# An mLSTM over a sequence of two chunks: the second chunk reads the first by its scores, without a state

## The chip, the core and the metric

The kernel runs on one core of one Trainium2 chip. A core has five engines that run side by side, each with its own list of instructions: TensorE (PE, matmuls into the accumulation memory PSUM), VectorE (DVE), ScalarE (ACT), GpSimd (POOL), and SyncE (SP), which here issues the transfers between the chip's main memory and the on-chip memory. Instructions of one engine run in order; engines wait for each other by semaphores. The metric is the device time of one execution in microseconds (us), the median of several.

## The reference, cut to what matters

One encoder layer is computed for two separate sequences, `x_prompt` with 1024 rows and `x_sample` with 256 rows, all in float32. Its second branch is an mLSTM in both directions with 4 heads of 256 channels. The sequence is cut into chunks of 128 rows; a state `C` (256x256) and `n` (256) is carried from chunk to chunk:

```python
def body(carry, inp):
    C, n, m = carry
    ...
    S = jnp.einsum('bhtd,bhsd->bhts', qc, kc) * Dexp
    num = jnp.einsum('bhts,bhsd->bhtd', S, vc) + inter_w[..., None] * jnp.einsum('bhtd,bhde->bhte', qc, C)
    den_raw = jnp.sum(S, axis=-1) + inter_w * jnp.einsum('bhtd,bhd->bht', qc, n)
    ...
    C_new = decay[..., None, None] * C + jnp.einsum('bhs,bhsd,bhse->bhde', w, kc, vc)
    n_new = decay[..., None] * n + jnp.einsum('bhs,bhsd->bhd', w, kc)
    return (C_new, n_new, m_new), h
```

The state starts at zero in each sequence and direction. `x_prompt` has 8 chunks, `x_sample` has 2. So in the short sequence only one state is ever used: the one that the first chunk leaves, read once by the second. There `qc` times `C_new` is `q (sum over s of w_s k_s v_s)`, which is the same number as `sum over s of (q k_s) w_s v_s`.

## The kernel before, in words

The kernel has three stages: the input projections (line 770, up to about 1168 us of the trace), the mLSTM stage (about 1168 to 1457 us), and the output projections (lines 1530 to 1532 and 1742 to 1744).

In the mLSTM stage the ten chunks are numbered 0 to 7 (long sequence) and 8, 9 (short). `qT`, `kT` hold q and k by channel (transposed), `vN` holds v by rows with a column of ones and one of zeros added (258 columns, so that `n` rides along), each in three pieces: chunks 0 to 4, 5 to 7, and 8, 9. Rows of k are loaded once more by chunk into small tiles `k` (six buffers).

A `Sweep` is one head in one direction. For every chunk it first takes a query, then makes a state:

- `query` (line 1357): two matmuls, q of the chunk times the state C, into the PSUM tile `qc` (one buffer); ACT scales it into `kept` or `qcf`.
- `state` (lines 1369 to 1383): a load of the rows of k, a scaling of v on ACT into `wv` (four buffers), two matmuls k times wv into the PSUM tile `u` (one buffer, line 1375), and on DVE a copy (line 1381, first state of a sequence) or decay and sum (line 1383) into the next C.

Two sweeps run per head: the first one's queries are kept, the second one runs ten steps later together with `Pairs`, which makes the scores inside a chunk (line 1418), weights and normalizes them, multiplies them with v (line 1458), transposes the result (line 1505), gates it into `og` on DVE (line 1508) and stores it to `ym_dr`. Heads 0 and 1 begin their first sweep with the short sequence (chunk 9, then 8), heads 2 and 3 end it there.

Between these small matmuls a `Filler` puts the matmuls of another product (lines 1597 to 1599, tiles `acc`): 32 units of 24 matmuls with 320 columns, each unit closed by a DVE step (line 589) that needs a tile `th`, loaded from `th_dr`. Two units can be open at a time.

The order of all this is not written out by hand. Each operation is recorded on a `Board` with an engine, a cost in us, what it reads and writes, and a step; `order` then plays a greedy list schedule over these costs, and every engine, SP with its loads among them, gets its instructions in that order. So a change in recorded operations can move others. Transfers all go through SP's queue.

Near the end of the stage `first_ym` loads parts of `ym_dr` back into `th` tiles and splits them for the next stage (ACT line 1618, DVE line 1619, tiles `y`).

Of the kernel before, what the change touches and what calls it, by code (L numbers as in the profile page):

```python
# [9 lines left out]
F32 = mybir.dt.float32  # L10
# [171 lines left out]
def encoder_kernel(  # L182
# [1153 lines left out]
    class Sweep:  # L1336


        def __init__(self, h, d, p):
            self.h, self.d, self.i, self.p, self.C = h, d, h % 2, p, None  # L1340
            self.order, self.first, self.has_state, self.has_query = [], set(), set(), set()
            for c0, n in SEQS[::1 - 2 * d]:
                cs = list(range(c0, c0 + n))[::1 - 2 * d]
                self.order += cs
                self.has_state.update(cs[:-1])
                self.has_query.update(cs[1:])
                self.first.add(cs[0])

        def query(self, c, dst, tok):
            if c not in self.has_query:  # L1350
                return
            i, C = self.i, self.C
            pq = buf(psM, [P, 512], F32, "qc", 1)

            def mm():
                for kd in range(2):
                    PE.matmul(pq[:, 0:HD + 2], qTs[i][:, kd, c * P:(c + 1) * P], C[:, kd, :], start=kd == 0, stop=kd == 1)  # L1357

            op("PE", .88, mm, r=[(qTs[i], piece(c)), C], w=[pq])
            op("ACT", .47, lambda: A.activation(dst(), pq[:, 0:HD + 2], AF.Copy, bias=0.0,  # L1360
                                                scale=gcol[:, 1, self.d, self.h, c:c + 1]), r=[pq], w=[tok])

        def state(self, c):
            if c not in self.has_state:
                return
            i, n, h = self.i, piece(c), self.h
            k, wv = buf(mp_, [P, HD], F32, "k", 6), buf(mp_, [P, HD + 2], F32, "wv", 4)
            load(128, lambda: k[:], kn_dr[c * P:(c + 1) * P, h * HD:(h + 1) * HD], (), [k])
            op("ACT", .51, lambda: A.activation(wv[:], vNs[i][:, c, :], AF.Copy, bias=0.0,
                                                scale=gcol[:, 3, self.d, h, c:c + 1]), r=[(vNs[i], n)], w=[wv])  # L1370
            pu = buf(psM, [P, 2, 512], F32, "u", 1)

            def mm():
                for db in range(2):
                    PE.matmul(pu[:, db, 0:HD + 2], k[:, db * P:(db + 1) * P], wv[:], start=True, stop=True)  # L1375

            op("PE", .88, mm, r=[k, wv], w=[pu])
            C0 = self.C
            C1 = self.C = buf(mp_, [P, 2, HD + 2], F32, f"C{self.p}", 2)
            if c in self.first:  # L1380
                op("DVE", .7, lambda: V.tensor_copy(C1[:], pu[:, :, 0:HD + 2]), r=[pu], w=[C1])
            else:
                op("DVE", .76, lambda: V.scalar_tensor_tensor(
                    out=C1[:], in0=C0[:], scalar=decay[:, self.d, h, c:c + 1], in1=pu[:, :, 0:HD + 2],
                    op0=ALU.mult, op1=ALU.add), r=[pu, C0], w=[C1])
# [251 lines left out]
    for s in range(10 * NH + 15):  # L1637
        board.step = s
        if s == 0:
            fills.unit(())  # L1640
            load_head(0, 2, "v")
        h, c, i = second(s - 3)
        if h is not None and h + 2 < NH and c in (5, 7, 9):
            load_head(h + 2, (5, 7, 9).index(c))
        h, i = divmod(s, 10)
        mark = len(board.ops)
        if h < NH:
            c, d = one[h].order[i], one[h].d
            one[h].query(c, lambda h=h, c=c, d=d: kept[h % 2][:, slot(d, c), :], (kept[h % 2], c))
            one[h].state(c)  # L1650
        if s == 0:
            fills.unit(())
            for n in DOWN:
                load_head(0, n, "q" if n == 2 else "qv")
            fills.unit(())
            fills.unit(())
        h, c, i = second(s)
        if h is not None:
            g = c - c % 2
            if i % 2 == 0:  # L1660
                prs[h, g] = Pairs(h, g, two_[h].d)
            two_[h].query(c, *prs[h, g].inter(c))
            two_[h].state(c)
            prs[h, g].scores(c)
            if i % 2:
                prs[h, g].factors()
        h, c, i = second(s - 2)
        if h is not None:
            prs[h, c - c % 2].values(c)
        h, c, i = second(s - 4)  # L1670
        if h is not None and i % 2 == 0:
            prs[h, c - c % 2].finish()
        if s in (3, 5):
            for h, n in ((0, 0), (1, 2), (1, 1)) if s == 3 else ((1, 0), (0, 1), (0, 2)):
                load_head(h, n, "qkv" if h else "k")
        after = [o for o in board.ops[mark:] if o.eng == "PE"][:1]
        while fills.at < PACE[s]:
            fills.unit(after)
        if s == 45:
            ym0 = [first_ym(0)]  # L1680
# [175 lines left out]
```

## Time and profile before

| | us |
|---|---|
| device time, median of 3 | 1698.51 |
| lowest, highest | 1695.8, 1698.83 |
| span of the profiled execution, first to last instruction | 1694.4 |
| PE busy in that span | 1654.8 |
| DVE, ACT, POOL busy | 1000.7, 577.4, 678.6 |

The profile is one execution; its own device time is not listed beside its span. A row of a group of instructions reads: line, engine, operation, output tile <- input tiles, shape, count, then busy us and mean ns of one, then the idle time of the engine just before them and what ended it. A float32 matmul shows as two records, so "x4" at a query is one query of two matmuls. A row of the timeline reads: start, duration, engine, line, operation, and in brackets the idle time of the engine before it with what ended that. DMA stands for a transfer, SPq for its issue.

### The profile page before, as it was taken

What the parts mean: (1) busy time and instruction counts of PE and PEld (TensorE: products, weight loads), DVE (VectorE), ACT (ScalarE), POOL (GpSimd) and SP (SyncE); (2) the same over time, 40 slices, a digit from 0 to 9 for tenths busy, and PEclk for the clock granted to TensorE, in tenths of its full rate; (3) what the DMA queues carried; (4) which work ended last, traced back from release to release, by engine and by line L of the source; (5) the groups of instructions that cost most, each with busy time, mean ns of one, the idle gap of its engine ahead of it and who ended that gap; (6) DMA issues with size and microseconds to landing.
All of it is one profiled execution on the core that took longest, in us unless ns stands there. A gap on an engine that the chain in (4) does not pass through costs nothing.

```text
span 1694.4 us, 27722 instructions
## 1 busy us (share of the span) xinstructions
PE 1654.8 (98%) x10542; PEld 1567.3 (92%) x10542; DVE 1000.7 (59%) x1696; ACT 577.4 (34%) x1117; POOL 678.6 (40%) x499
## 2 busy tenths in 40 slices
PE   7999999999999999999999999999999999999997
PEld 2799999999999999999999999999988899998985
DVE  4794434456555565566656886652267777565645
ACT  3552332124453222222222211212256565333322
POOL 1133333335664566677666633333210101223412
PEclk9999999999999999999999999999999999999999
DMA  9334325324553122221222556468779855783631
GB/s 318 108 127 137 120 89 124 73 77 124 149 154 103 57 69 69 82 81 61 62 66 82 145 129 141 118 134 289 254 234 293 261 186 158 231 279 119 239 108 63
DMA packets 282681, 241.88 MB, mean 143 GB/s; under 512 B 96196, under 2 KB 237748, under 8 KB 282548
## 3 DMA queue, kind: packets, MB, share of 16 engines
q1 hardware_dynamic: 282368, 240.06, 46.6%
q8 instruction: 84, 1.38, 0.3%
q14 instruction: 49, 0.40, 0.1%
q10 hardware_dynamic: 180, 0.04, 0.0%
HBM read 171.16 MB, written 68.89 MB: 142 GB/s over the span
## 4 chain that ended last, share of the span: by engine, by line
PE 90%; DVE 4%; DMA 3%; SPq 1%; issue 1%; ACT 1%; ACTq 0%; DVEq 0%
PE acc L770 61%; PE qc L1357 3%; PE u L1375 3%; PE accd L1530 2%; PE accd L1531 2%; PE accd L1532 2%; PE accd L1743 2%; PE accd L1744 2%; PE accd L1742 2%; PE acc L1598 2%; PE acc L1597 2%; PE acc L1599 2%; DMA raw<-in_w_in_dram 1%; PE misc L1418 1%; SPq L318 1%; PE misc L1458 1%
## 5 line engine op out<-in xcount | busy, mean ns | idle before, releaser
L330 POOL TENSOR_TENSOR wl<-comb,wh 128x512 fp32r<-128x512 f32 x176 | 247.3, 1405 | 288.0 <-ACT wh L329 279.8
L686 DVE TENSOR_TENSOR q<-acc,q 128x640 f32<-128x640 f32 x272 | 220.8, 819 | 221.5 <-PE acc L770 219.3
L330 POOL TENSOR_TENSOR wl<-raw,wh 128x512 fp32r<-128x512 f32 x136 | 191.8, 1411 | 237.0 <-ACT wh L329 225.2
L770 PE MATMUL acc<-xt,wh 128*128 128x320 f32 x1408 | 265.1, 310 | 2.2 <-DVE xt L382 2.2
L770 PEld LDWEIGHTS acc<-xt,wh 128*128 128x128 f32 x1408 | 220.9, 188 | 3.5 <-DVE xt L382 3.2
L329 ACT CAST wh<-comb 128x512 fp32r<-128x512 f32 x176 | 109.0, 619 | 298.5 <-PE acc L770 282.6
L329 ACT CAST wh<-raw 128x512 fp32r<-128x512 f32 x136 | 84.4, 621 | 271.0 <-PE acc L770 205.5
L770 PE MATMUL acc<-xt,wl 128*128 128x320 f32 x704 | 160.3, 309 | 0.0
L1558 POOL TENSOR_TENSOR wl<-raw,wh 128x512 fp32r<-128x512 f32 x28 | 36.2, 1297 | 233.4 <-ACT wh L1557 227.0
L770 PEld LDWEIGHTS acc<-xt,wl 128*128 128x128 f32 x704 | 117.7, 188 | 0.0
L642 DVE TENSOR_TENSOR comb<-raw 128x512 f32<-128x512 f32 x88 | 73.4, 834 | 41.1 <-DMA raw<-in_w_in_dram 19.1
L837 POOL TENSOR_TENSOR big<-big,q 128x640 f32<-128x640 f32 x48 | 78.3, 1631 | 35.8 <-DVE q L686 27.4
L586 ACT ACTIVATE q<-q,zero 128x640 f32<-128x640 f32 x76 | 63.1, 831 | 78.0 <-DVE q L686 72.3
L642 DVE TENSOR_TENSOR comb<-raw,comb 128x512 f32<-128x512 f32 x44 | 46.0, 1045 | 62.6 <-POOL wl L330 62.6
L770 PE MATMUL acc<-b00H,wh 128*128 128x320 f32 x352 | 81.6, 312 | 0.0
L1530 PE MATMUL accd<-y,wh 128*128 128x320 f32 x256 | 79.9, 313 | 1.5 <-DVE og L1508 1.5
L770 PE MATMUL acc<-b10H,wh 128*128 128x320 f32 x352 | 80.2, 308 | 0.8 <-ACT q L700 0.8
L770 PE MATMUL acc<-b11H,wh 128*128 128x320 f32 x352 | 80.7, 310 | 0.0
L770 PE MATMUL acc<-t2H,wh 128*128 128x320 f32 x352 | 80.4, 310 | 0.0
L770 PE MATMUL acc<-t3H,wh 128*128 128x320 f32 x352 | 80.3, 309 | 0.0
L770 PE MATMUL acc<-t3L,wh 128*128 128x320 f32 x352 | 80.2, 309 | 0.0
L770 PE MATMUL acc<-t3H,wl 128*128 128x320 f32 x352 | 80.2, 309 | 0.0
(307 smaller groups left out, 4144.0 us busy)
## 6 DMA issues: line engine op xcount, KB each, us to landing
raw<-in_w_in_dram SPq DMA_DIRECT2D x108, 256.0 KB
raw<-in_w_in_dram SPq DMA_DIRECT2D x40, 512.0 KB
th<-th_dr SPq DMA_DIRECT2D x32, 320.0 KB
th_dr<-q SPq DMA_DIRECT2D x28, 320.0 KB
raw<-in_w_proj_conv_dram SPq DMA_DIRECT2D x16, 512.0 KB
k<-kn_dr SPq DMA_DIRECT2D x64, 128.0 KB
raw<-in_w_proj_mlstm_dram SPq DMA_DIRECT2D x16, 512.0 KB
raw<-in_w_out_dram SPq DMA_DIRECT2D x16, 512.0 KB
```

The costliest lines, as they stand in the source:

```text
L329: op("ACT", .63, lambda: A.copy(wh[:], src()), r=r, w=[wh])
L330: op("POOL", 1.4, lambda: G.tensor_tensor(out=wl[:], in0=src(), in1=fp(wh[:]), op=ALU.subtract), r=[*r, wh], w=[wl])
L586: A.activation(out, in_, AF.Tanh, bias=zero[:, 0:1], scale=0.5)
L642: op("DVE", .9, lambda: V.tensor_tensor(out=t[:], in0=x(), in1=y(), op=o), r=[x.tok, y.tok], w=[t])
L686: op("DVE", .82, lambda: V.tensor_tensor(out=two(dst()), in0=acc[:, :, 0:TQ], in1=two(t()), op=ALU.add), r=[acc, t.tok], w=[dst.tok])
L770: PE.matmul(acc[:, q, 0:TQ], st_[:, k_, :], m_[:, q * TQ:(q + 1) * TQ], start=k_ == 0 and n == 0, stop=k_ == 3 and n == 2)
L837: op("POOL", 1.65, lambda: G.tensor_tensor(out=dst(), in0=dst(), in1=t(), op=ALU.mult), r=[dst.tok, t.tok], w=[dst.tok])
L1357: PE.matmul(pq[:, 0:HD + 2], qTs[i][:, kd, c * P:(c + 1) * P], C[:, kd, :], start=kd == 0, stop=kd == 1)
L1375: PE.matmul(pu[:, db, 0:HD + 2], k[:, db * P:(db + 1) * P], wv[:], start=True, stop=True)
L1530: PE.matmul(accs[q][:, :TQ], wh, yH, start=kt == 0, stop=False)
L1531: PE.matmul(accs[q][:, :TQ], wh, yL, start=False, stop=False)
L1558: op("POOL", 1.36, lambda wh=wh, wl=wl, src=src: G.tensor_tensor(out=wl[:], in0=src(), in1=fp(wh[:]), op=ALU.subtract), r=[raw, wh], w=[wl])
```

## The change

For the sequence of two chunks, in each head and direction, the state is no longer made. Where the first chunk made it, `crossed` multiplies k of this chunk with q of the other one (two matmuls with 128 columns, accumulated in the PSUM tile `u`), and ACT scales the rows of this score matrix by the weights w of the keys while it copies it into a `wv` buffer, 128 columns wide. The second chunk's query is then one matmul of these weighted scores with v of the first chunk, 258 columns, into `qc`. The load of the rows of k, the scaling of v and the DVE copy go, for this sequence. The loads of head 0 at the start of the stage change with it: all of q, k and v of chunks 8 and 9 come first.

```diff
+                if n == 2:
+                    self.short = cs
 
         def query(self, c, dst, tok):
...
-            op("PE", .88, mm, r=[(qTs[i], piece(c)), C], w=[pq])
+            if c == self.short[1]:
+                w, c0 = self.w, self.short[0]
+                op("PE", .46, lambda: PE.matmul(pq[:, 0:HD + 2], w[:, 0:P], vNs[i][:, c0, :], start=True, stop=True),
+                   r=[w, (vNs[i], piece(c0))], w=[pq])
+            else:
+                op("PE", .88, mm, r=[(qTs[i], piece(c)), C], w=[pq])
...
+        def crossed(self, c):
+
+            i, t = self.i, self.short[1]
+            pu, self.w = buf(psM, [P, 2, 512], F32, "u", 1), buf(mp_, [P, HD + 2], F32, "wv", 4)
+            w = self.w
+
+            def mm():
+                for kd in range(2):
+                    PE.matmul(pu[:, 0, 0:P], kTs[i][:, kd, c * P:(c + 1) * P], qTs[i][:, kd, t * P:(t + 1) * P],
+                              start=kd == 0, stop=kd == 1)
+
+            op("PE", .45, mm, r=[(kTs[i], piece(c)), (qTs[i], piece(t))], w=[pu])
+            op("ACT", .29, lambda: A.activation(w[:, 0:P], pu[:, 0, 0:P], AF.Copy, bias=0.0,
+                                                scale=gcol[:, 3, self.d, self.h, c:c + 1]), r=[pu], w=[w])
 
         def state(self, c):
             if c not in self.has_state:
                 return
+            if c == self.short[0]:
+                return self.crossed(c)
...
         if s == 0:
             fills.unit(())
-            load_head(0, 2, "v")
+            load_head(0, 2)
...
-            for n in DOWN:
-                load_head(0, n, "q" if n == 2 else "qv")
+            for n in DOWN[1:]:
+                load_head(0, n, "qv")
...
-            for h, n in ((0, 0), (1, 2), (1, 1)) if s == 3 else ((1, 0), (0, 1), (0, 2)):
+            for h, n in ((0, 0), (1, 2), (1, 1)) if s == 3 else ((1, 0), (0, 1)):
```

The list schedule gives three places another order that matter below. The first is SP at the start of the mLSTM stage, the loads of head 0 (`raw` and `th` belong to the filler; a piece of the difference):

```order
 L318 DMA raw<-in_w_proj_conv_dram 128x4x256 x2
 L318 DMA th<-th_dr 128x640
-L318 DMA k<-kn_dr 128x256
 L318 DMA qT<-qT_dr 128x2x256
+L318 DMA kT<-kT_dr 128x2x256
 L318 DMA vN<-v_dr 128x3x256
 L318 DMA qT<-qT_dr 128x2x384
```

The load of the rows of k went, kT of chunks 8 and 9 came in behind qT. On PE the first state product stood behind two filler units (48 matmuls), its query another two units later; the first score product now stands behind two and a half units (60), its use one and a half units later.

The second is PE where head 1's first sweep begins with the short sequence while head 0's second sweep begins with chunk 0 (lines 1357 and 1375 are 1359 and 1399 in the changed kernel, 1378 and 1363 the new ones). Before:

```order
L1599 MATMUL acc<-b10H,wl 128x320
L1357 MATMUL qc<-C_12258,qT 128x258 x2
L1375 MATMUL u<-wv,k 128x258 x4
L1357 MATMUL qc<-C_12406,qT 128x258 x2
L1597 MATMUL acc<-b00H,wh 128x320
```

and now:

```order
L1623 MATMUL acc<-b10H,wl 128x320
L1359 MATMUL qc<-C_12252,qT 128x258 x2
L1378 MATMUL u<-qT,kT 128x128 x2
L1363 MATMUL qc<-vN,wv 128x258
L1399 MATMUL u<-wv,k 128x258 x2
```

Between the score product and the matmul that uses it, by way of ACT, PE has nothing else here. In the other seven cases at least filler, a transpose or a product of the other sweep stands between the two.

The third is the end of the stage on ACT (`y` parts are casts for the next stage, `qcf<-qcf,rstm` is the last scaling, ahead of the last transposes on PE). Before:

```order
L1476 ACTIVATE junk,ssqm_11832<-qcf,zero 128x256
L1486 ACTIVATE rs_r<-ssqm_11832,zero 128x2
L1618 CAST y_14977<-th 128x640
L287 CAST wh<-raw 128x512
L1498 ACTIVATE qcf<-qcf,rstm_11834 128x256 x2
L1618 CAST y_14977<-th 128x640
```

and now:

```order
L287 CAST wh<-raw 128x512
L1510 ACTIVATE rs_r<-ssqm_11832,zero 128x2
L1642 CAST y_14948<-th 128x640 x2
L287 CAST wh<-raw 128x512
L1522 ACTIVATE qcf<-qcf,rstm_11834 128x256 x2
L1642 CAST y_14948<-th 128x640
```

One more cast of y stands ahead of the last scaling; on DVE, in the same way, one more part of y stands ahead of the last `og`. On PE, between the last value product and the last transposes, 24 filler matmuls stood, and now 18; the six stand earlier, between the last score product and the transpose behind it.

## The prediction

> **What bounds the kernel now.** I read the page's busy times first, then the table by stages, then the waits of PE in the stage that the change touches.
>
> ```profile
> span 1694.4 us, 27722 instructions
> PE 1654.8 (98%) x10542; PEld 1567.3 (92%) x10542; DVE 1000.7 (59%) x1696; ACT 577.4 (34%) x1117; POOL 678.6 (40%) x499
> ```
>
> PE is busy for 98% of the span, no other engine for more than 59%. An average says little of one stage, so here is the mLSTM stage, which is the only one whose instructions change (windows from 1168 to 1455 us; columns: length, then busy time of PE, PEld, DVE, ACT and POOL, the granted clock, the DMA share, GB/s):
>
> ```profile
> 1168.00:1455.00 287.00, 278.55 (x1637) 254.28 (x1637) 174.99 (x584) 148.59 (x387) 40.93 (x36) 1.00 0.73 235
> 1320.00:1390.00 70.00, 69.29 (x396) 61.82 (x395) 52.78 (x186) 43.71 (x120) 5.09 (x4) 1.00 0.71 226
> 1390.00:1455.00 65.00, 63.68 (x406) 59.86 (x404) 47.85 (x167) 36.33 (x98) 12.77 (x10) 1.00 0.55 171
> ```
>
> PE is idle for 8.4 of these 287 us. The filler product, which is spread between the small matmuls of the recurrence, covers nearly every round trip over DVE and ACT. The waits of PE between 1168 and 1460 us say where the idle time is (in total, times, longest):
>
> ```profile
> PE u L1375 <- DMA th<-th_dr: 2.1, 1, 2.1
> PE accd L1530 <- DVE og L1508: 1.5, 1, 1.5
> PE qc L1357 <- DVE C L1383: 1.4, 2, 0.9
> PE u L1375 <- ACT wv L1369: 0.8, 1, 0.8
> PE qc L1357 <- ACT kept L1360: 0.5, 2, 0.3
> ```
>
> The largest stand at the two ends of the stage. So, in this stage, a microsecond of matmul that is not issued should be a microsecond of span, as long as the order still covers the round trips.
>
> **The change part by part.** *What PE no longer does, and what it does instead.* The recurrence on PE consists of two groups, and two present groups have the shapes of what is added (busy us, mean ns; one float32 matmul shows as two records):
>
> ```profile
> L1375 PE MATMUL u<-wv,k 128*128 128x258 f32 x256 | 67.4, 386 | 3.9 <-DMA th<-th_dr 2.1 <-ACT wv L1369 0.8 <-PE misc L1418 0.5
> L1357 PE MATMUL qc<-C,qT 128*128 128x258 f32 x256 | 66.8, 383 | 2.0 <-DVE C L1383 1.4 <-ACT kept L1360 0.5
> L1418 PE MATMUL misc<-kT,qT 128*128 128x128 f32 x160 | 24.1, 274 | 0.0
> 1195.14 0.87 PE qc L1357 x4
> 1196.01 0.87 PE u L1375 x4
> 1292.77 0.45 PE misc L1418 x4
> 1298.14 0.45 PE misc L1458 x2
> ```
>
> The means overlap, since matmuls are pipelined; the last four rows, from the chain of waits, give what each takes of PE's time. A state update (four records) is 0.87 us, a query 0.87 us, a score product of 128x128 over two halves 0.45 us, one matmul with 256 columns 0.45 us. The short sequence is met once for each of 4 heads and 2 directions, so 8 times. Removed: 8 x (0.87 + 0.87) = 13.9 us. Added: 8 x (0.45 + 0.44) = 7.1 us, where 0.44 is half of a query. Net: 6.8 us less. It cannot be much more, since this is all that PE issues less; it becomes less where PE waits instead.
>
> *What the other engines no longer do.* Eight copies of a state (L1381) leave DVE, eight scalings of 258 columns (L1369) become scalings of 128 columns read from PSUM, of which a copy like L1456 is the nearest:
>
> ```profile
> L1381 DVE COPY C<-u 128x516 f32<-128x516 f32 x16 | 11.1, 691 | 4.3 <-PE u L1375 4.2
> L1369 ACT ACTIVATE wv<-vN,gcol 128x258 f32<-128x258 f32 x64 | 31.5, 506 | 24.5 <-PE u L1375 16.1 <-DMA raw<-in_w_proj_conv_dram 5.8 <-DMA vN<-v_dr 2.4
> L1456 ACT COPY Ps<-misc 128x128 f32<-128x128 f32 x40 | 10.6, 264 | 19.3 <-PE misc L1455 18.5
> ```
>
> That is 5.5 us of DVE and 1.9 us of ACT, and eight loads of k (128 KB each). PE's 278.55 of 287 us hide DVE's 174.99 and ACT's 148.59, so I cost these savings at nothing. Between update and query a copy of 0.69 us used to stand; now it is a scaling of about 0.27. The round trip that PE must cover becomes shorter.
>
> *The start of the stage.* The first crossing needs q and k of the last two chunks by columns, not rows of k, so SP loads kT (256 KB by its shape) behind qT, and the k load (128 KB) in front of them goes. The rows are from the timeline: issues on SP, then the instructions that show a landing.
>
> ```profile
> 1170.84 0.46 SPq L318 DMA_DIRECT2D th<-th_dr  x1
> 1176.89 0.62 ACT L1557 CAST wh<-raw 128x512 fp32r<-128x512 f32 x1 [0.87 <-DMA raw<-in_w_proj_conv_dram]
> 1177.76 0.88 DVE L589 SCALAR_TENSOR_TENSOR th<-th,acc 128x320 f32<-128x320 f32 x2 [9.05 <-DMA th<-th_dr]
> 1178.21 1.11 PE L1375 MATMUL u<-wv,k 128*128 128x258 f32 x4 [2.11 <-DMA th<-th_dr]
> 1179.92 1.31 ACT L1369 ACTIVATE wv<-vN,gcol 128x258 f32<-128x258 f32 x3 [2.41 <-DMA vN<-v_dr]
> 1185.42 0.49 DVE L589 SCALAR_TENSOR_TENSOR th<-th,acc 128x320 f32<-128x320 f32 x1 [5.37 <-DMA th<-th_dr]
> ```
>
> The first th lands at about 1177.7. Behind it in the queue came k 128, qT 256 and vN 384 KB, and vN was there at 1179.9: 768 KB in 2.2 us, about 345 GB/s, in the order of issue. In the changed order kT ends 512 KB behind th: 512/345 = 1.5, so at 1179.2. PE now does half a filler unit (12 matmuls of 0.147 us, 1.8 us) after the same wait for th, which DVE frees at 1177.76 + 0.49 = 1178.25 instead of 1178.21, and reaches the crossing at about 1180.1. Slack 0.9 us; no wait. All later loads move back by 128 KB, 0.37 us: the second th to 1185.8, its DVE step to 1186.3, just when PE, which has 0.85 us less to do there, wants that accumulator (1186.2). Loss at the start with the 0.04 from above: 0.1 us. From below it cannot be under 0; from above it is 5.4, if the loads land together (rival below).
>
> *The second crossing.* Here the order gives PE nothing between the scores and their use. Before, PE waited at this place too:
>
> ```profile
> 1231.14 0.48 ACT L1360 ACTIVATE kept<-qc,gcol 128x258 f32<-128x258 f32 x1 [0.34 <-PE qc L1357]
> 1232.80 1.11 PE L1375 MATMUL u<-wv,k 128*128 128x258 f32 x4 [0.83 <-ACT wv L1369]
> ```
>
> The scaling now stands behind the 0.48 us of kept on ACT, as two scalings of v did before. From the query's end it is 0.48 for kept, 0.27 for the scaling and three hand-overs, which I put at 0.05 each as an estimate: 0.9, of which the scores cover 0.45. Wait about 0.5 instead of 0.83: gain 0.3 us, at least 0, at most 0.8. At the other six the order puts 0.9 us or more of PE work between scores and use (a transpose, a state update, filler), against about 0.4 for a free ACT; I cost them at nothing. If each were uncovered it would cost what the uncovered waits above cost, 0.3 to 0.8 us each (rival).
>
> *The seam at the end.* The last value product, the transposes behind it and the first matmul of the next stage:
>
> ```profile
> 1450.41 0.67 PE L1458 MATMUL misc<-vN,Ps 128*128 128x256 f32 x2 [0.18 <-DVE og L1508]
> 1451.08 0.14 PE acc L1597
> 1454.45 0.16 PE acc L1599
> 1454.89 0.95 PE L1505 MATMUL misc<-ident,qcf 128*128 128x128 f32 x4 [0.30 <-ACT qcf L1498]
> 1457.30 0.64 PE L1530 MATMUL accd<-y,wh 128*128 128x320 f32 x1 [1.46 <-DVE og L1508]
> ```
>
> From value product to transposes it is 4.48 us by way of DVE and ACT, and PE waits 0.30 at the end although 24 filler matmuls (1451.08 to 1454.61, 0.147 each) stand in between. In the changed order only 18 do; six moved ahead of an earlier transpose, where PE was busy. So 6 x 0.147 = 0.9 us of filler covers nothing any more: loss 0.9. In addition ACT and DVE now take one more part of y ahead of the last scaling and of the last og. The second and third part stood at
>
> ```profile
> 1454.34 0.90 ACT L1498 ACTIVATE qcf<-qcf,rstm 128x256 f32<-128x256 f32 x2
> 1455.42 0.73 ACT L1618 CAST y<-th 128x640 fp32r<-128x640 f32 x1 [0.18 <-DMA th<-ym_dr]
> 1456.38 0.86 DVE L1508 SCALAR_TENSOR_TENSOR og<-misc,mhq,og 128x256 f32<-128x256 f32 x2
> ```
>
> A cast of 0.73 us ahead of the scaling would push the transposes by up to 0.7, but og was held until 1456.38 by an earlier part of y on DVE, a microsecond after the transposes; so most of it hides there. I take 0.2, with 0 and 1.5 (the part's load late as well) as ends.
>
> *Sum.* 6.8 - 0.1 + 0.3 - 0.9 - 0.2 = 5.9 us. The profiled execution would become 1694.4 - 5.9 = 1688.5 us of span. Its own device time is not listed; the three timed executions (1695.8, 1698.51, 1698.83) lie 1.4 to 4.4 us above its span. I take the 4.1 us of the median as what lies around it: **1692.6 us**, 0.35% faster. This median is near the top of its three, so 1 us less would not surprise.
>
> **The rivals.** *The clock.* The granted clock fell once near here:
>
> ```profile
> 1179.00:1190.00 11.00, 11.00 (x74) 10.86 (x73) 1.67 (x3) 3.44 (x7) 2.57 (x2) 1.00 1.07 373
> 1457.00:1458.00 1.00, 0.70 (x3) 0.70 (x3) 1.00 (x2) 0.00 (x0) 1.00 (x1) 0.52 0.98 200
> 1460.00:1461.00 1.00, 1.00 (x7) 1.00 (x6) 0.00 (x0) 0.00 (x0) 0.00 (x0) 0.77 1.04 400
> 1461.00:1462.00 1.00, 1.00 (x9) 1.00 (x8) 0.00 (x0) 0.48 (x1) 0.00 (x0) 1.00 1.12 413
> ```
>
> After the seam PE ran at half clock from 1457.3 to about 1460.5; half of 3.2 us, 1.6 us, was lost. After the idle 2.1 us at the start of the stage it did not fall. The change makes PE's idle stretch at the seam longer by about a microsecond and leaves the one at the start as it is, so I expect the same picture. If the clock stays up at the seam: 1691.0 us. If it also falls at the start: 1694.2.
>
> [...]
>
> *Round trips eat the saving.* If the six crossings with cover, which I cost at nothing, wait 0.3 to 0.8 us each because ACT is in the middle of something else (kept, a transposed copy, a filler cast of 0.62), the loss is about 6 x 0.55 = 3.3 us: 1695.9 us, no change that can be told. For it: ACT is in order, and the scaled scores hold one of the four wv buffers until their query, so a later scaling of v, and all behind it on ACT, can wait. Against: in the waits above PE waited for ACT for 0.8 + 0.5 us in 287, with 128 updates and queries.
>
> *Slower: the first crossing is starved.* If the loads issued after th share the rate instead of landing in order, kT lands with the second th at 1185.4. PE would stand from 1180.1 on for 5.3 us, and behind so long a gap the clock falls as at the seam, 1.6 us more: 5.9 - 6.9 = -1.0, so 1699.5 us, slower. Behind it on ACT stand three scalings of v and two filler casts (1.31 + 2 x 0.62 = 2.5 us); if the filler weights are late for that, 1702.0. It decides once kT is some 5 us later than 1179.2. Against it: the landings 1177.7, 1179.9 and 1185.4 fit one queue in order.
>
> That the change does not do what it says is excluded by the order: eight score products, eight single products with v, eight k loads fewer.
>
> **How the numbers follow.** My forecast gets 0.60 (own range 1690.5 to 1694.5), the open clock 0.08, the second fall 0.07, the round trips 0.18, the starved start 0.07. This kernel's measurement can tell about 0.2%, 3.4 us, from no change: faster means under 1695.1, slower over 1701.9. Faster: the first three less 0.04 for the upper edge of the forecast, 0.71. Same: that edge, the round trips and 0.03 of the starved start, 0.25. Slower: the starved start with late filler weights, 0.04. The range, 1689.3 to 1697.0, takes in the forecast, both cases of the clock and the round trips.
>
> **What would show it.** Right: 256 - 32 = 224 records on each of the two lines of the recurrence; PE busy in the stage down by about 6.5 us and PE idle up by 1 or less; PE's wait before the last transposes 1.0 to 1.5 us; the next stage starts about 5.9 us earlier. Wrong: waits of PE on the scaled scores of over 1 us in sum; a wait of the first score product on qT or kT; a half clock near the start of the stage; or stalls at places where the order merely shifted.

## The result, and the profile after

| | kernel before | changed kernel |
|---|---|---|
| device time, median of 8 runs each | 1697.42 us (1695.8 to 1698.83) | 1692.47 us (1691.43 to 1694.06) |
| ratio, 95% interval | | 0.9974 (0.9966 to 0.9983) |
| span of the profiled execution | 1694.4 us | 1690.3 us |

The changed kernel is faster by 0.26%, and the predicted 1692.6 us is 0.1 us off. That looks better than it is: two errors of about a microsecond cancelled. The working took 5.9 us off a median of three runs, 1698.51; over eight runs the kernel before has 1697.42, 1.1 us less. The gain was not 5.9 either: 4.95 us by the medians, 4.1 us by the two spans. The traces say where the rest of the spans' difference went. First the page of the changed kernel (busy times by engine):

```profile
span 1690.3 us, 27664 instructions
PE 1648.8 (98%) x10526; PEld 1562.4 (92%) x10526; DVE 989.9 (59%) x1688; ACT 575.0 (34%) x1117; POOL 677.2 (40%) x499
```

PE is busy for 6.0 us less (1654.8 before), DVE for 10.8, ACT for 2.4; the span is 4.1 shorter. The working had 5.5 us of DVE; part of the rest is steps that last longer beside other work in one trace than in the other (the subtractions y<-th,y take 9.2 us in all before and 6.5 now). The groups of the recurrence on PE, with the two new lines last:

```profile
L1399 PE MATMUL u<-wv,k 128*128 128x258 f32 x224 | 58.6, 384 | 0.4 <-ACT wv L1393 0.4
L1359 PE MATMUL qc<-C,qT 128*128 128x258 f32 x224 | 58.5, 383 | 1.9 <-DVE C L1407 1.4 <-ACT kept L1367 0.3 <-ACT qcf L1367 0.2
L1378 PE MATMUL u<-qT,kT 128*128 128x128 f32 x32 | 5.0, 279 | 0.5 <-DVE C L1407 0.5
L1363 PE MATMUL qc<-vN,wv 128*128 128x258 f32 x16 | 4.9, 387 | 0.5 <-ACT wv L1382 0.5
```

32 records fewer on each of the old lines, 48 on the new ones. The waits of PE from 1164 to 1460 us (total, times, longest):

```profile
PE misc L1529 <- ACT qcf L1522: 3.0, 1, 3.0
PE acc L1621 <- DVE th L589: 1.8, 1, 1.8
PE qc L1359 <- DVE C L1407: 1.4, 2, 0.9
...
PE accd L1554 <- DVE og L1532: 0.6, 1, 0.6
...
PE qc L1363 <- ACT wv L1382: 0.5, 1, 0.5
```

The first row is new in size: before the last transposes PE waited 0.3 us, now 3.0. It is the seam between this stage and the next: the chain from the last value product to the first matmul of the next stage. Here are its instructions in the changed kernel, from its timeline over all engines (start, duration, then engine, line and operation, and the idle time ahead with what ended it):

```profile
1444.37 0.59 PE L1482 MATMUL misc<-vN,Ps 128*128 128x256 f32 x2
...
1446.59 0.29 ACT L1510 ACTIVATE rs_r<-ssqm,zero 128x2 f32<-128x2 f32 x1
...
1447.64 0.49 DVE L589 SCALAR_TENSOR_TENSOR th<-th,acc 128x320 f32<-128x320 f32 x1 [1.26 <-PE acc L1623]
1448.05 0.16 DVE L1513 RECIPROCAL rs_r<-rs_r 128x2 f32<-128x2 f32 x1
...
1448.72 1.26 POOL L288 TENSOR_TENSOR wl<-raw,wh 128x512 fp32r<-128x512 f32 x1 [0.67 <-ACT wh L287]
1448.83 1.17 DVE L1517 TENSOR_TENSOR rstm<-rs_t,rs_r 128x2 f32<-128x2 f32 x1
...
1450.04 0.91 ACT L1522 ACTIVATE qcf<-qcf,rstm 128x256 f32<-128x256 f32 x2 [1.39 <-DVE rstm L1517]
1450.60 1.30 PE L1529 MATMUL misc<-ident,qcf 128*128 128x128 f32 x4 [3.00 <-ACT qcf L1522]
...
1452.48 0.64 PE L1554 MATMUL accd<-y,wh 128*128 128x320 f32 x1 [0.58 <-DVE og L1532]
```

Two things stand out. The DVE step of the last filler unit (L589) now stands ahead of the reciprocal, whose input was there at 1446.88; DVE waited for PE until 1447.64. And the last step on DVE (L1517), 0.16 us long in the kernel before, lasted 1.17 us and ended within 0.02 us of POOL's subtraction of weights (1449.98). The clock, in windows of half a microsecond (length, busy time of PE, PEld, DVE, ACT, POOL, granted clock, DMA share, GB/s):

```profile
1449.50:1450.00 0.50, 0.00 (x0) 0.00 (x0) 0.50 (x2) 0.00 (x0) 0.48 (x1) 0.90 0.83 170
1450.00:1450.50 0.50, 0.00 (x0) 0.00 (x0) 0.50 (x2) 0.47 (x2) 0.00 (x0) 0.50 0.76 201
...
1456.00:1456.50 0.50, 0.50 (x4) 0.50 (x3) 0.15 (x1) 0.00 (x0) 0.00 (x0) 0.50 0.91 300
...
1457.00:1457.50 0.50, 0.50 (x5) 0.50 (x5) 0.00 (x0) 0.00 (x0) 0.00 (x0) 1.00 1.10 350
```

It is at half from 1449.90 to about 1456.73, 6.8 us, where before it was for 3.4.

The stage can be cut in three by marks that every trace has: the first DVE step of the stage (the first th has landed), the last value product, and the first matmul of the next stage.

| us | before | changed | difference | the working had |
|---|---|---|---|---|
| first DVE step to last value product | 272.65 | 266.86 | -5.8 | -6.1 |
| last value product to next stage | 6.89 | 8.11 | +1.2 | +0.2 |
| next stage to end | 237.1 | 237.8 | +0.7 | 0 |

The missing 0.25 us of the 4.1 lie ahead of the first of these marks.

The -6.1 is the working's 6.8 - 0.1 + 0.3 = 7.0 of saving, less the 0.9 of filler that it had moving ahead of the last value product. By this table the saving is there; the seam lost more than it was costed at, and so did the next stage.

### The profile page after: what moved, and what is told of

Its sections match the earlier page's. It is cut to its first block, busy times and chain, and to the rows that moved or that the text cites. A ratio compares the mean times of both kernels' runs of the same rounds, so it can differ in the third digit from the quotient of the medians.

```text
span 1690.3 us, 27664 instructions
## 1 busy us (share of the span) xinstructions
PE 1648.8 (98%) x10526; PEld 1562.4 (92%) x10526; DVE 989.9 (59%) x1688; ACT 575.0 (34%) x1117; POOL 677.2 (40%) x499
## 4 chain that ended last, share of the span: by engine, by line
PE 89%; DMA 4%; DVE 4%; SPq 1%; ACT 1%; issue 1%; ACTq 0%; DVEq 0%
PE acc L770 62%; PE u L1399 3%; PE qc L1359 2%; PE accd L1554 2%; PE accd L1555 2%; PE accd L1556 2%; PE accd L1767 2%; PE accd L1768 2%; PE accd L1766 2%; PE acc L1622 2%; PE acc L1621 2%; PE acc L1623 2%; DMA raw<-in_w_in_dram 1%; SPq L318 1%; PE misc L1482 1%; DVE xt L387 1%
## 5 line engine op out<-in xcount | busy, mean ns | idle before, releaser
L330 POOL TENSOR_TENSOR wl<-raw,wh 128x512 fp32r<-128x512 f32 x136 | 190.6, 1402 | 236.3 <-ACT wh L329 224.4
L770 PE MATMUL acc<-xt,wh 128*128 128x320 f32 x1408 | 265.0, 310 | 2.2 <-DVE xt L382 2.2
```

The lines of the kernel that those rows point to most:

```text
L330: op("POOL", 1.4, lambda: G.tensor_tensor(out=wl[:], in0=src(), in1=fp(wh[:]), op=ALU.subtract), r=[*r, wh], w=[wl])
L770: PE.matmul(acc[:, q, 0:TQ], st_[:, k_, :], m_[:, q * TQ:(q + 1) * TQ], start=k_ == 0 and n == 0, stop=k_ == 3 and n == 2)
```

## The experiments

*The theory:* PE's work sets the time of the stage, so the saving is the matmul time; what is missing of it was lost at the seam by DVE's order, by a hold between DVE and POOL (the step on DVE that lasted 1.17 us in place of 0.16 and ended within 0.02 us of POOL's subtraction), and by the clock. *Rivals:* the gain comes from DVE and ACT work or a shorter round trip; the seam is long for another reason (casts, late parts of y); the loss lies at the start of the stage. Medians below are each compared with the runs of the kernel before on the same chip.

**1. The crossing's matmuls twice.**

```diff
-  lambda: PE.matmul(pq[:, 0:HD + 2], w[:, 0:P], vNs[i][:, c0, :], ...)
+  lambda: [PE.matmul(pq[:, 0:HD + 2], w[:, 0:P], vNs[i][:, c0, :], ...) for _ in range(2)]
-  for kd in range(2):          # scores
+  for kd in (0, 1, 0, 1):
```

> The changed kernel with both matmul groups of each crossing issued twice (the same result, the order on every engine the same). If PE's work sets the time of this stage, 8 x (0.45 + 0.44) = 7.1 us come back: about 1699.6 us against 1692.5 for the changed kernel, so 1 to 3 us above the kernel before, and PE's busy time is 7.1 us higher. If the gain came from a shorter round trip or from DVE and ACT, the repeated matmuls fall into time in which PE waits, and the time stays under 1695.

1698.54 us, ratio 1.0003 (0.9994 to 1.0012): the whole gain is gone. On the page:

```profile
PE 1656.0 (98%) x10574; PEld 1570.0 (93%) x10574; DVE 994.1 (59%) x1688; ACT 574.8 (34%) x1117; POOL 679.8 (40%) x499
```

PE is busy 7.2 us more than in the changed kernel, the span is 1695.2, 4.9 us more, and the stretch to the last value product 271.97 against 266.15 (mean of the seven executions with the changed kernel's work and order in it). So 5.8 of 7.1 us came back as span in the stage. The waits on DVE and ACT stayed what they were. That PE's work carries the gain, but for what experiment 2 leaves open, is shown; one repeated crossing costs 0.73 us in this stretch rather than the 0.89 of the price list, and the median is 0.6 us over that of the kernel before, below the 1 to 3 us that were expected.

**2. Work put back on DVE and ACT.**

```diff
+  A.activation(w[:, P:HD + 2], vNs[i][:, c, P:HD + 2], AF.Copy, bias=0.0, scale=1.0)
+  V.tensor_copy(C1[:], vNs[i][:, min(c, t):min(c, t) + 2, :])
```

> The changed kernel with the work put back that the change took from DVE and ACT, as idle work beside each crossing: a copy of 128x516 on DVE (8 x 0.69 = 5.6 us) and a scaling of 130 columns on ACT (8 x about 0.3 us). PE's order is the same. If these savings were hidden, as the prediction costed them, nothing changes: 1692.5, at most 1 us more. If the saved DVE and ACT time was part of the gain, 2 us or more come back: 1694.5 or over.

1694.40 us, ratio 0.9980 (0.9971 to 0.9989), where the changed kernel has 0.9974 and, in a second series, 0.9976: 0.7 to 1.0 us more, with intervals that overlap. That fits "hidden, at most 1 us"; a fraction of a microsecond can't be told from nothing here. It does not give back the 2 us that the rival needs, but the test is weaker than it was meant to be: the copy, which reads v from SBUF, takes 0.42 us and not 0.69, so 3.4 of DVE's 5.5 us were put back (and 2.4 us on ACT for 1.9). In its profiled execution the stretch up to the last value product is 268.37 us, 2.2 over the mean in experiment 1. Two waits of PE are longer there: 1.2 us for the load of b00L (0.7 and 0.4 in two executions of the changed kernel), and 0.7 us for a scaling of v whose load came late, as for 1.5 us in experiment 4, where nothing was added to ACT or DVE. So I do not count the 2.2 us as their work; that up to about 1 us of the gain is theirs stays open.

**3. The seam's order mended.** The last filler step goes behind the reciprocal square root, three casts of y behind the last scaling, their subtractions behind the last og.

```diff
+  fills.step.before.add(board.newton)
+  for o in [o for o in board.ops[mark:] if o.eng in ("ACT", "DVE")][2:]:
+      o.before.add(board.scaled if o.eng == "ACT" else board.gated)
```

> The changed kernel, with the order at the end of the stage mended on DVE and ACT: the DVE step of the last filler unit stands behind the last reciprocal square root, the last three casts of y behind the last scaling, their subtractions behind the last og. If what stood ahead of the reciprocal (1.2 us of waiting for the last filler unit) made the seam long, PE's wait before the last transposes falls from 3.0 to about 1.8 us and the first matmul of the next stage comes 1.2 to 1.6 us earlier: about 1691.1. If the wait has another cause (a cast of weights on ACT, a subtraction on POOL), it stays near 3.0 and the time at 1692.5. If the later y parts are missed in the next stage, 0.5 to 1 us of the gain goes again there.

1694.34 us, ratio 0.9979 (0.9969 to 0.9989): no gain in time, although this profiled execution has a span of 1689.3. From the last value product to the next stage it is 7.65 us, 0.46 less than in the changed kernel. What took the rest, from DVE's and POOL's timelines:

```profile
1446.10 0.17 DVE L1513 RECIPROCAL rs_r<-rs_r 128x2 f32<-128x2 f32 x1 [0.54 <-ACT rs_r L1510]
1446.30 0.94 DVE L1514 TENSOR_TENSOR rs_t<-rs_r 128x2 f32<-128x2 f32 x1
1447.28 0.16 DVE L1515 TENSOR_TENSOR rs_t<-rs_t,ssqm 128x2 f32<-128x2 f32 x1
1447.47 1.24 DVE L1516 TENSOR_SCALAR rs_t<-rs_t 128x2 f32<-128x2 f32 x1
...
1445.95 1.28 POOL L288 TENSOR_TENSOR wl<-raw,wh 128x512 fp32r<-128x512 f32 x1 [5.87 <-ACT wh L287]
1447.43 1.26 POOL L288 TENSOR_TENSOR wl<-raw,wh 128x512 fp32r<-128x512 f32 x1 [0.20 <-ACT wh L287]
```

The reciprocal starts as soon as its input is there, so the first half of the theory holds. But then two steps on two columns take 0.94 and 1.24 us, and both end when a subtraction on POOL ends (1447.23 and 1448.69). PE's wait fell to 2.71 us, not to 1.8, and the next stage now waits 0.4 us for a part of y.

**4. Idle matmuls in the seam.** 15 products of 128x128, 11 ahead of the last transposes and 4 behind.

```diff
+  op("PE", .23, lambda: PE.matmul(acc[:, 0:P], ident[:], ident[:], start=True, stop=True), w=[acc], after=after)
```

> The changed kernel with 15 idle matmuls of 128x128 on PE, about 0.22 us each, 11 between the last filler unit and the last transposes and 4 behind the transposes; the other engines' order is the same. If the granted clock falls at the seam because PE has too little work there, it stays at 1.00: the transposes take 0.6 instead of 1.3 us and the next stage starts without 4 us of half clock, 2.0 to 2.6 us less in all: about 1690.2. If the clock falls all the same, the time stays at 1692.5. If the idle matmuls come to stand in the way, it is slower by up to 1 us.

1692.27 us, ratio 0.9968 (0.9956 to 0.9979): by the ratios 1.0 to 1.4 us under the changed kernel, not the 2.0 to 2.6 that were expected. The clock does not fall:

```profile
1450.00:1454.00 4.00, 3.38 (x29) 3.00 (x28) 3.82 (x9) 1.96 (x4) 1.73 (x2) 1.00 0.54 142
1454.00:1458.00 4.00, 3.94 (x29) 3.75 (x28) 1.02 (x3) 0.73 (x1) 0.00 (x0) 1.00 1.03 359
```

From the next stage's start to the end it is 236.3 us, 1.5 less than in the changed kernel. The seam itself stays at 8.14 us, since the fixed chain over DVE and POOL is as long as before. So the whole half clock of the changed kernel costs about 1.5 us in the next stage, and with these matmuls, which keep PE busy for 3.38 of the 4 us from 1450, it does not come. The span, 1691.2, shows no gain, because this execution has the longest stretch of the seven, 267.61, with the late load of v in it.

**5. The changed kernel again**, beside the next three.

> The changed kernel once more, unchanged, on the same chip and beside the same runs of the kernel before as the next three. Expected 0.3% under the kernel before, a seam of 8.1 us from the last value product to the first matmul of the next stage, and the last step of the reciprocal square root on DVE stretched to about 1.2 us beside a subtraction on POOL.

1692.84 us, ratio 0.9976 (0.9966 to 0.9986), 3.9 us under the kernel before in this series, span 1690.2: a stretch of 265.95, the same seam (8.11) and the same half clock of 6.8 us. The seam belongs to the order, not to one execution.

**6. Other instructions for the square root.** As experiment 3, with the four steps behind the reciprocal as three scalar_tensor_tensor.

```diff
-  V.tensor_tensor(out=t[:], in0=r[:], in1=r[:], op=ALU.mult)
-  ...
+  V.scalar_tensor_tensor(out=t[:], in0=r[:], scalar=-0.5, in1=r[:], op0=ALU.mult, op1=ALU.mult)
+  V.scalar_tensor_tensor(out=t[:], in0=t[:], scalar=1.0, in1=sv, op0=ALU.mult, op1=ALU.mult)
+  V.scalar_tensor_tensor(out=rv, in0=t[:], scalar=1.5, in1=r[:], op0=ALU.add, op1=ALU.mult)
```

> The kernel with the mended order at the seam, and the four steps of the reciprocal square root behind the reciprocal written as three scalar_tensor_tensor on DVE. In the mended kernel two of the four steps (a tensor_tensor and a tensor_scalar) lasted 0.94 and 1.24 us instead of 0.16 and ended when POOL's subtraction of weights ended. If tensor_tensor and tensor_scalar are held while POOL works on a tensor, and scalar_tensor_tensor is not, each step takes 0.16 to 0.2 us, the last scaling starts 1.7 us earlier, and PE's wait before the last transposes falls from 2.7 to about 1.0 us; the time is 1.7 us under the mended kernel, less up to 1 us if a y part is then late. If any DVE work is held beside POOL, the steps stay as long in sum (2.5 us) and nothing is gained.

1692.48 us, ratio 0.9974 (0.9965 to 0.9983); the expectation fails:

```profile
1448.75 0.17 DVE L1513 RECIPROCAL rs_r<-rs_r 128x2 f32<-128x2 f32 x1 [0.54 <-ACT rs_r L1510]
1448.95 0.94 DVE L1514 SCALAR_TENSOR_TENSOR rs_t<-rs_r 128x2 f32<-128x2 f32 x1
...
1450.13 1.23 DVE L1516 SCALAR_TENSOR_TENSOR rstm<-rs_t,rs_r 128x2 f32<-128x2 f32 x1
...
1448.60 1.28 POOL L288 TENSOR_TENSOR wl<-raw,wh 128x512 fp32r<-128x512 f32 x1 [5.86 <-ACT wh L287]
1450.08 1.26 POOL L288 TENSOR_TENSOR wl<-raw,wh 128x512 fp32r<-128x512 f32 x1 [0.20 <-ACT wh L287]
```

The kind of instruction is not what matters. What the held ones have in common is that all their tensors lie in SBUF, and in this run two are read; the reciprocal, with one, passes at 1448.75 while POOL is at work.

**7. The intermediate values in PSUM.** As experiment 3; in the last square root of the stage alone, each step reads at most one tensor from SBUF.

```diff
+  V.reciprocal(r_, r[:])          # r_, t_ in PSUM
+  V.reciprocal(r[:], r[:])
+  V.scalar_tensor_tensor(out=t_, in0=r_, scalar=-0.5, in1=r[:], op0=ALU.mult, op1=ALU.mult)
+  V.scalar_tensor_tensor(out=t_, in0=t_, scalar=1.0, in1=sv, op0=ALU.mult, op1=ALU.mult)
+  V.scalar_tensor_tensor(out=rv, in0=t_, scalar=1.5, in1=r[:], op0=ALU.add, op1=ALU.mult)
```

> The kernel with the mended order at the seam; in the last reciprocal square root of the stage alone, the intermediate values lie in PSUM, so that each of its steps reads at most one operand from SBUF (one more reciprocal in all); the order on every engine is the same. [...] If any DVE instruction is held beside POOL, the steps stay at 2.5 us in sum.

1690.37 us, ratio 0.9957 (0.9944 to 0.9969), span 1686.4: the lowest median of all, below both kernels, though its interval still touches that of the changed kernel (0.9966 to 0.9983).

```profile
1446.84 0.17 DVE L1520 SCALAR_TENSOR_TENSOR qc<-qc,rs_r 128x2 f32<-128x2 f32 x1
1447.04 0.17 DVE L1521 SCALAR_TENSOR_TENSOR qc<-qc,ssqm 128x2 f32<-128x2 f32 x1
1447.24 0.16 DVE L1522 SCALAR_TENSOR_TENSOR rstm<-qc,rs_r 128x2 f32<-128x2 f32 x1
...
1446.28 1.28 POOL L288 TENSOR_TENSOR wl<-raw,wh 128x512 fp32r<-128x512 f32 x1 [5.87 <-ACT wh L287]
...
1448.14 0.95 PE L1540 MATMUL misc<-ident,qcf 128*128 128x128 f32 x4 [1.03 <-ACT qcf L1533]
```

All three steps run in 0.17 us each inside POOL's 1446.28 to 1447.56. PE's wait is 1.03 us (2.71 in experiment 3), the seam 5.96, and the clock stays at 1.00. The wait for the last y part is 0.2 us. By the ratios the time is 3.7 us under that of experiment 3: 1.7 us in the seam, and 1.6 us from the next stage to the end (236.53 against 238.10), which runs without a half clock here. Of the steps beside POOL, those with two operands in SBUF lasted 0.94 and 1.23 us (experiments 3 and 6), and with one of them in PSUM 0.16 to 0.17. The tensor_scalar of experiment 3 lasted 1.24 us beside POOL with only one tensor read; why, no run tests.

**8 and 9. Both kernels with one mended end.** The order of experiment 3 with the second of the four y parts left ahead of the last og, the steps of experiment 6, and the subtractions of y as scalar_tensor_tensor: once on the changed kernel, once on the kernel before.

```diff
-  for o in [o for o in board.ops[mark:] if o.eng in ("ACT", "DVE")][2:]:
+  for o in [o for o in board.ops[mark:] if o.eng in ("ACT", "DVE")][4:]:
-  V.tensor_tensor(out=y[1][:, k], in0=raw[:], in1=fp(y[0][:, k]), op=ALU.subtract)
+  V.scalar_tensor_tensor(out=y[1][:, k], in0=raw[:], scalar=1.0, in1=fp(y[0][:, k]), op0=ALU.mult, op1=ALU.subtract)
```

> As the kernel with scalar_tensor_tensor steps, with the subtractions of y in the same form too, and the second y part of the last four back ahead of the last scaling and og, so that the next stage finds it in time. Expected: PE's wait before the last transposes about 1.0 us, from the last value product to the next stage's first matmul 6.0 us instead of 8.1, the granted clock not lower for longer than in the changed kernel: 2 to 4 us under the changed kernel, about 1689.5. If the next stage then waits for its y parts, half of that is given back.

> The kernel before (a state between the two chunks) with the same three edits at the seam as the kernel expected at 1689.5. If the change is worth its saved PE work (6.8 us) once both have the same end of the stage, this one is 6.5 to 7.3 us slower than that: about 1696.5, near the kernel before (one DVE step of y shorter, so up to 0.5 us faster). If the loss against the sum lies elsewhere than at the seam, the distance stays at the 4 to 5 us of the two original kernels.

1691.75 us, ratio 0.9969 (0.9957 to 0.9980), and 1695.54 us, ratio 0.9994 (0.9985 to 1.0003). Their distance is 3.8 us by the medians and 5.8 by the spans (1688.5 and 1694.3; 0.6 us of the 5.8 lies ahead of the first DVE step of the stage), less than the 6.5 hoped for; by the medians it is no more than that of the two original kernels, which was the other expected case. So the pair does not show what equal ends would give, since the ends did not become equal. The stretch up to the last value product is 265.78 against 271.90: 6.1 us, the working's number. The seams still differ, 7.45 against 6.36 us, because the steps of the square root fall beside POOL's subtraction in the one and ahead of it in the other. The wait before the transposes was 2.5 us, not 1.0, for the reason that experiment 7 then showed.

**10. Four buffers for th and y.** Experiment 7 with four buffers in place of three.

```diff
-  th = buf(thp, [P, TH2], F32, "th", 3)
+  th = buf(thp, [P, TH2], F32, "th", 4)
```

> The same, with four instead of three buffers for the halves of th and the y parts, so that the last y part is loaded ahead of the seam (the order of the recurrence shifts at a few places too). Expected: PE's wait before the last transposes about 1.0 us, no wait for a y part in the next stage, 1.7 us less from the last value product to the next stage than in the mended kernel and at most one stretch of half clock: 2 to 4 us under the changed kernel, about 1689.5. If the shifted order costs more waits in the recurrence, they show there and the gain is less.

1692.73 us, ratio 0.9967 (0.9956 to 0.9979): 2.4 us over the median with three, with intervals that overlap, and 4.0 us over its span. There is no wait before the transposes (the seam of 7.25 us has more filler in it), but the shifted order starves the second crossing:

```profile
1232.43 0.42 SPq L318 DMA_DIRECT2D kT<-kT_dr  x1
...
1237.81 1.19 PE L1378 MATMUL u<-qT,kT 128*128 128x128 f32 x4 [6.54 <-issue]
```

PE waits 6.5 us, and the clock is at half from 1234.6 to 1241.4. No releaser is shown; with three buffers the kT load of this head was issued at 1217.32, here at 1232.43, so I take it to be kT. That is the outcome of the prediction's slow rival (a crossing that is starved by its load), at the second crossing instead of the first and for another reason: the load was issued late, while the rival had loads that share the rate.

**11. The crossing in the first sweeps only.**

```diff
-  self.short = cs
+  self.short = [None, None] if p else cs
```

> The changed kernel with the direct crossing in the first sweep of each head only (4 of 8); the second sweeps keep a state between the two chunks. The change's loads are kept. If the gain is PE's work, half of it: the stretch from the first DVE step of the stage to the last value product, 272.3 us on average before and 266.2 after, is 3.0 to 3.6 us shorter than before, so about 269; the time is 1 to 3 us under the kernel before, by what the seam's order costs here. If one place alone (the second crossing, or one wait) makes the gain, the stretch is near 266 or near 272.

1703.34 us, ratio 1.0028 (1.0016 to 1.0040): slower than both kernels, against the theory's number and the rivals' too. The matmul counts are as meant (16 and 8 records on the new lines), but the list schedule made another order of it. Its first wait and what followed, and its seam:

```profile
1445.98 0.33 PE L1479 MATMUL misc<-ident,Pt 128*128 128x128 f32 x1 [2.03 <-DVE Pt L1476]
...
1443.60:1447.00 3.40, 1.37 (x9) 1.02 (x8) 3.03 (x10) 2.27 (x7) 0.35 (x1) 1.00 0.37 134
1447.00:1450.50 3.50, 3.50 (x15) 3.32 (x13) 2.05 (x8) 1.51 (x4) 0.00 (x0) 0.51 0.64 159
...
1459.81 0.95 PE L1529 MATMUL misc<-ident,qcf 128*128 128x128 f32 x4 [3.47 <-ACT qcf L1522]
```

A wait of 2.0 us shortly before the end was followed by a half clock of 3.4 us, and the seam, 8.41 us, by a second one of 6.8. The stretch is 275.2 us instead of 269: 2.0 of the 6.2 are this wait and about 1.7 the clock; 2 to 3 us I can't place. So this run does not test the proportion, and shows that the order alone can cost more than the change is worth.

**12. The changed load order in the kernel before.**

```diff
-  load_head(0, 2, "v")
+  load_head(0, 2)
-  for n in DOWN: load_head(0, n, "q" if n == 2 else "qv")
+  for n in DOWN[1:]: load_head(0, n, "qv")
```

> The kernel before with the changed order of loads at the start of the stage alone (q and k of the last two chunks by columns ahead of the rows of k). If the start costs 0.1 us as predicted, the time is that of the kernel before within 1 us, and the stretch from the first DVE step to the last value product is 272 to 273 us. If the order of loads starves the start, PE waits there for a load for 1 us or more.

1697.80 us, ratio 1.0001 (0.9993 to 1.0010): the loads cost nothing that can be measured. The stretch is 273.76, 1.5 us over the other two executions of the old work (272.65 and 271.90), because in this execution the clock fell at the start too, the other branch of the prediction's clock rival:

```profile
1179.50:1180.00 0.50, 0.31 (x2) 0.34 (x3) 0.44 (x2) 0.00 (x0) 0.50 (x1) 1.00 1.09 348
1180.00:1180.50 0.50, 0.50 (x5) 0.50 (x4) 0.00 (x0) 0.00 (x0) 0.21 (x1) 0.73 1.10 357
...
1183.00:1183.50 0.50, 0.50 (x4) 0.50 (x3) 0.00 (x0) 0.27 (x1) 0.00 (x0) 0.50 1.17 389
```

## Why the prediction was right or wrong, point by point

- *PE bounds the stage: right.* Repeating the crossing's matmuls took the whole gain away, and putting 3.4 us back on DVE and 2.4 on ACT cost 0.7 to 1.0 us by the ratios.
- *PE's work, 6.8 us: right.* Its price list (0.87, 0.87, 0.45, 0.44) gave -6.1 for the stretch up to the last value product. The mean of seven executions with the new work (after, again, the mended seams and the idle matmuls) is 266.15 us, of two with the old 272.3 (without the one whose clock fell at the start): -6.1. The single ones scatter, from 265.0 to 267.6, so the agreement to a tenth is luck; to half a microsecond it is not.
- *DVE, ACT and loads of k at nothing: right within what was measured*, 0 to 1 us, with only part of DVE's work put back.
- *The start, 0.1: right.* In the changed kernel PE waited for th, not for kT:

```profile
1178.14 0.38 PE L1621 MATMUL acc<-b00H,wh 128*128 128x320 f32 x1 [1.85 <-DVE th L589]
...
1179.98 0.61 PE L1378 MATMUL u<-qT,kT 128*128 128x128 f32 x4
```

  The crossing at 1179.98 (1180.1 in the working) has no wait ahead of it.
- *The second crossing, 0.3: right.* The wait on the scaling was 0.46 us, 0.5 in the working, 0.83 before. The scaling takes 0.36 us on the mean, not 0.27. Of the other crossings one waited 0.5 us, ahead of its scores, for the PSUM buffer that a state update on DVE still read; the rival of round trips is out.
- *The seam, 0.9 + 0.2: the step that failed.* The 0.9 was right: 18 filler matmuls are left, and the other six lie in the stretch before. The 0.2 was too small: from the last value product to the next stage it is 1.2 us more. The working looked at the casts of y on ACT and the og on DVE. It did not look at the filler's DVE step, which the order had put ahead of the reciprocal, and it took a step of 0.16 us for 0.16 us wherever it stands. The reciprocal began 1.17 us after its input was there, and the held step was 1.0 us too long. From the square root's end to rstm's end it was 0.98 us before and 3.12 after; 0.5 us of that was hidden by ACT, which before was still busy with casts, and 0.5 by og. Two of the prediction's own signs missed with it: PE's wait before the last transposes is 3.0 us and not 1.0 to 1.5, and the next stage starts 4.8 us earlier and not 5.9.
- *The clock, no change: wrong by 0.7 to 1.0 us.* It fell earlier in the longer gap and stayed at half for 6.8 us instead of 3.4. "The same picture" was the wrong reading. What sets the length, no run shows: experiment 2, with the same order and a seam of 7.94 us, had 3.4 us of half clock, and experiment 6, with a seam of 7.44, had 6.8.
- *The slow rival* did not happen. A crossing that waits for its load is possible all the same: in experiment 10, where the load was issued late, one waited 6.5 us.

Sum by the runs: -6.1 + 1.2 + 0.9 = -4.0 us, against 4.1 and 4.2 by the spans of the changed kernel's two profiled executions and 4.95 and 3.9 by the medians of the two series. The prediction's 5.9 missed the seam's 1.0 and the clock's 0.9.

## What to carry to other kernels

Where one engine is busy for 97% of a stage, a price list of its instructions from the chain of waits forecast the change of work here within the scatter of single executions; what it did not forecast is what the new order of the list schedule does at the stage's last dependency chain, so walk that chain step by step on every engine, with what stands ahead of each instruction. A DVE step on two columns with two operands in SBUF took 0.16 us here, and 0.30 to 1.26 in 62 of the 63 cases in which it began while a subtraction ran on GpSimd: on a chain that ends a stage, keep one operand in PSUM (0.16 to 0.17 us in experiment 7) or GpSimd's work elsewhere. And compare orders, not only work: half of this change came out in another order and was slower than none of it.

## What the runs showed of the hardware that was not expected

**Steps on DVE and POOL lasted longer side by side.** The kernel before has it too, away from the chain that counts: on DVE's timeline a subtraction of y that takes 0.82 us elsewhere lasted 1.92, and ended 0.69 us after POOL's of the same time, which ended at 1449.18.

```profile
1447.95 1.92 DVE L1619 TENSOR_TENSOR y<-th,y 128x640 fp32r<-128x640 f32 x1
...
1447.71 1.47 POOL L288 TENSOR_TENSOR wl<-raw,wh 128x512 fp32r<-128x512 f32 x1 [1.59 <-ACT wh L287]
```

POOL's subtractions lasted longer as well, 1.47 us here against 1.26 to 1.28 in the rows above: one in experiment 9 took 1.89 us, and one in experiment 12, which began at 1440.09, 0.21 us behind the start of a subtraction of y on DVE, took 1.77. And the hold is not peculiar to the seam. In the 14 traces, 63 DVE steps on two columns that read two tensors in SBUF began while a subtraction ran on POOL: 62 took 0.30 to 1.26 us and ended 0.02 us after it, and one, which began within 0.01 us of it, took its usual 0.16. None of the 771 that began at other times took over 0.17, and none of the 57 reciprocals, with one tensor read, that began beside such a subtraction.

**The clock was at half for 3.4 or 6.8 us.** In 14 profiled executions the stretches of half clock in and behind this stage were 3.4 us (before, experiments 2, 3, 8, 9, 12 and the first of 11) or 6.8 (the changed kernel twice, experiments 1, 6, 10 and the second of 11), none between; experiments 4 and 7 had none. In experiment 11 the two falls, at 1447.06 and 1460.71, are 13.65 us apart, and in experiment 12, at 1180.23 and 1460.13, 279.90 us. PE was not idle ahead of them: for 1.37 of the 3.40 us ahead of the first fall in experiment 11 it was busy. Here are the 3.41 us ahead of the fall and the half clock in the kernel before, the same and the time behind it in the changed kernel, and a piece of the half clock in experiment 2 (columns as in the table by windows above):

```profile
1453.62:1457.03 3.41, 1.85 (x11) 1.16 (x9) 2.56 (x6) 2.87 (x6) 1.56 (x2) 1.00 0.23 85
1457.04:1460.45 3.41, 3.15 (x12) 3.15 (x13) 1.65 (x2) 0.00 (x0) 0.97 (x1) 0.50 1.01 305
...
1446.49:1449.90 3.41, 1.11 (x8) 0.85 (x6) 2.12 (x6) 2.16 (x5) 2.47 (x2) 1.00 0.16 41
1449.90:1453.31 3.41, 2.14 (x7) 1.52 (x8) 2.48 (x5) 0.91 (x2) 0.08 (x1) 0.50 0.97 312
1453.31:1456.72 3.41, 3.41 (x15) 3.41 (x14) 0.83 (x1) 0.72 (x1) 0.00 (x0) 0.50 0.97 332
1456.73:1460.14 3.41, 3.41 (x25) 3.41 (x24) 0.49 (x1) 0.28 (x1) 0.00 (x0) 1.00 0.97 272
...
1455.57:1458.98 3.41, 3.27 (x12) 3.27 (x13) 0.09 (x1) 0.15 (x1) 0.00 (x0) 0.50 1.02 340
```

Behind 1.85 us of PE's work in the kernel before and 1.11 us in the changed one the clock fell. In the changed kernel it stayed at half behind 2.14 us and came back behind 3.41; in the kernel before it came back behind 3.15. The length of a wait of PE alone does not tell it: at the start of the stage the clock fell behind a wait of 2.34 us in experiment 12, the only one of the 14 with a fall there, and did not behind one of 2.53 us in experiment 11. Apart from experiment 4, where more matmuls on PE went with a clock that stayed up, these runs do not show what makes it fall, or for how long.
